# Deeper weight splitting in the up product of a hybrid encoder layer, and three reorderings around it

## The chip, the cores and the metric

The kernel runs on one core of a Trainium2 chip. The metric is the device time of one launch in microseconds (us), lower is better. A core has five engines that work side by side, each through its own queue in program order: TensorE (PE; its weight loads are shown as PEld), VectorE (DVE, `V` in the code), ScalarE (ACT, `A`), GpSimd (POOL, `G`) and SyncE (SP), which here issues nearly all DMAs. An engine that waits for something holds up all that stands behind it in its queue.

## The reference

One layer of an encoder trunk is applied to two batches (prompt and sample) of 512 tokens of width 1024, with shared weights, all in float32:

```python
xn = _rmsnorm(x, norm1_g); proj = xn @ w_in
a_out = (gelu(lru_gate) * (h_fwd + h_bwd)) @ w_lru_out      # RG-LRU in both directions
b_out = o.reshape(B, S, ATT_OUT) @ w_att_out                # dilated window attention, three groups
x = x + (sigmoid(g_a) * a_out + sigmoid(g_b) * b_out) @ w_o
xn2 = _rmsnorm(x, norm2_g)
gate, val = jnp.split(xn2 @ w_up, 2, axis=-1)
x = x + (gelu(_dwconv(gate, ffn_conv_w, ffn_conv_b)) * val) @ w_down
```

w_up is 1024 x 6144, w_down 3072 x 1024, w_o 1024 x 1024.

## The kernel before

**Split weights.** A product of float32 matrices is made of three matmuls of a faster type: every operand is split into a high part (hi, a cast) and a low part (lo, the difference), and hi*hi, hi*lo and lo*hi are added up in a PSUM bank. A weight slab (128 x 512, 256 KB) is loaded into a raw buffer (four of them) by SP, its hi is cast by ACT (L227) and its lo subtracted by an engine from the list `lo_eng` (L230), which is rotated at each split. hi and lo have eight buffers each.

**The stream.** All slabs stand in one list, in the order of their use, and the class `Stream` (L64) hands them out. `adv(n)` splits up to n more slabs, as long as fewer than eight are live; `take(n)` gives n to the caller and splits them first if it must; `done` says that n are used up. Loads are issued three places ahead of the splits. Since every engine works in program order, the place at which `adv` stands in the code fixes where the cast, the subtraction and the load stand in the queues of ACT, DVE or POOL, and SP. `hold` stops the splits at a given slab until it is raised.

**The stages around the change.** After the input projections and attention come, for batch 0 and then batch 1:

- mix (`mix_tile`, L985): eight tiles; each takes three slabs of w_lru_out and one of w_att_out, multiplies 30 + 12 matmuls into a double bank (two such banks), and DVE multiplies the gates on (L1000 to L1004). Gates come by `th_load` one tile ahead. The rows of x, onto which the output is added, come by `load_acc` (four DMAs of 512 KB): for batch 0 ahead of the mix, for batch 1 after its tile 3.
- output (`o_phase`, L1056, `o_group`, L1041): 16 groups of 12 matmuls, each added to the rows by DVE (L1054, called the residual's addition here). In batch 0 a hook after each group also splits batch 1's y (L846, L847), transposes its o (L886 to L889) and, in the last four groups, makes the second norm: `norm2_tile` (ACT squares, POOL takes the root, DVE scales by L1020 into an `x2s` buffer) and two groups later `norm2_T`, whose transposes give the operands B11 and B21 (L1037 to L1039).
- the last eight groups of batch 1 (L1173) have their own norm steps between them, in the table `after` (L1162): `own_sums` (store the rows, ACT squares them into a PSUM bank called junk), `own_scale`, and `sums`, whose transposes (L1122) and additions give the operands T1 to T4 and B22. In the last two of these groups each slab is given back as soon as it is used, and the first eight slabs of w_up are split there.

**The up product.** w_up's columns go in 24 steps f of 128 gate and 128 value columns, and seven products (Strassen's scheme in Winograd's form) do the work of eight: B11 and B21 (`batch0`, L1205), then T2, T1, T3, B22 and T4 (`rest`, L1218), 12 matmuls each (`prod`, L1188; matmuls L1195 to L1197). Their slabs are A11, A12, S2, S1, S3, S4, A22, of which four come from additions on DVE in `up_split` (L257): S1 = A21 + A22, S2 = S1 - A11 when A12 is split (for f < 4 when S2 is), S3 = A11 - A21 and S4 = A12 - S2, written over A21 and A12, when S2 is split. A21 has one buffer, A22 two, S1 and S2 one each. T2, T3 and T4 are added up in one bank (pfA), T1 and B22 in another (pfC); between T2 and T3 the bank is copied (u2, by ACT at L1229, for f = 2 and 3 by DVE), between T1 and B22 likewise (p5), and after T3 DVE adds it to p5 (L1236). After B22 come the gate (g1), a convolution over the tokens on DVE (L1243, L1245), gelu on ACT (L1247), two multiplications on DVE and the store f_d. For f < 4 B11 and B21 run ahead, while `sums` of the last rows is still under way; these are the `batch0(0)` to `batch0(3)` in front of the loop. After `batch0(2)` `hold` is raised and lo goes to POOL alone.

**The down product** follows (L1314 to L1316); at its start the first two f rows are fetched and split (`h_pair`, L1265), and rows of x come back from DRAM (accd).

Of the kernel before, what the change touches and what calls it, by code (L numbers as in the profile page):

```python
# [11 lines left out]
F32 = mybir.dt.float32  # L12
# [7 lines left out]
D = 1024  # L20
T = 1024
S = 512
# [91 lines left out]
def layer_kernel(ctx: ExitStack, tc: tile.TileContext, xs_in, norm1_g, w_in, conv_w, conv_b, lru_wa, lru_ba,  # L114
# [3 lines left out]
    V, A, G, PE, SP = nc.vector, nc.scalar, nc.gpsimd, nc.tensor, nc.sync  # L118
# [3 lines left out]
    def open_pool(name, side="left", **kw):  # L122
        cm = tc.tile_pool(name=name, bufs=1, side=side, reuse_waits="tile", **kw)
        return cm, cm.__enter__()
# [83 lines left out]
    hi_eng, lo_eng = ["dve"], [G]  # L208
# [69 lines left out]
    ws = Stream(specs, wload, wsplit, 3, {"a": 8, "b": 8})  # L278
# [3 lines left out]
    def wcol(slabs, j):  # L282
        return lambda k: slabs[k // 4][j][:, 128 * (k % 4):128 * (k % 4) + 128]
# [17 lines left out]
    for t in range(8):  # L301
        x_t = xi.tile([128, D], F32, name=f"xt{t}")
# [653 lines left out]
    cm_ps, ps3 = open_pool("ps3", space=PSUM)  # L956
# [3 lines left out]
    cm_m, mp = open_pool("mix")  # L960
# [3 lines left out]
    def load_acc(b):  # L964
        for i in range(4):
            acc[4 * b + i] = acp.tile([128, D], F32, tag=f"acc{i}", bufs=1, name="acc")
            SP.dma_start(out=acc[4 * b + i], in_=xs_in[b][0, 128 * i:128 * i + 128, :])
# [4 lines left out]
    def half_pair(pool, nm, **kw):  # L972
        return tuple(pool.tile([128, 4, S], F32R, name=nm, tag=nm + hl, bufs=1) for hl in "hl")
# [11 lines left out]
    def mix_tile(b, c):  # L985
        wa = ws.take(3)
        ps = ps3.tile([128, 2, 512], F32, tag="m", bufs=2, name="ps")
        mm3(ps[:, 0], wcol(wa, 0), wcol(wa, 1), lambda k: yh[k], lambda k: yl[k], KR)
        ws.done("a", 3)
        ws.adv(2)  # L990
        wb = ws.take(1)
        mm3(ps[:, 1], wcol(wb, 0), wcol(wb, 1), lambda k: oT["h"][:, k], lambda k: oT["l"][:, k], 4)
        ws.done("a", 1)
        ws.adv(2)
        if c + 1 < KD:
            th_load(b, c + 1)
        ta, tb = ths.pop((b, c, 0)), ths.pop((b, c, 1))
        mh = mbp.tile([128, S], F32R, tag=f"mh{c}", bufs=1, name="mh")
        ml = mbp.tile([128, S], F32R, tag=f"ml{c}", bufs=1, name="ml")
        V.scalar_tensor_tensor(out=ta, in0=ta, scalar=1.0, in1=ps[:, 0], op0=ALU.add, op1=ALU.mult)  # L1000
        V.scalar_tensor_tensor(out=tb, in0=tb, scalar=1.0, in1=ps[:, 1], op0=ALU.add, op1=ALU.mult)
        V.tensor_tensor(out=ta, in0=ta, in1=tb, op=ALU.add)
        act(out=mh, in_=ta, func=AF.Copy, scale=0.5)
        V.scalar_tensor_tensor(out=ml, in0=ta, scalar=0.5, in1=mh, op0=ALU.mult, op1=ALU.subtract)  # L1004
        mix[c] = (mh, ml)
# [17 lines left out]
    SP.dma_start(out=gain2, in_=norm2_g[0].partition_broadcast(128))  # L1023

    def norm2_tile(t):
        x_t = mp.tile([128, D], F32, tag="x2s", bufs=2, name="x2s")
        norm2_scale(t, x_t, norm2_sums(t, x_t), gain2)
        xst[t] = x_t

    def norm2_T(t):  # L1030
        x_t = xst.pop(t)
        tl = slice(128 * (t % 4), 128 * (t % 4) + 128)
        for kk in range(0, KD, 4):
            h, l = x2["B11" if kk == 0 else "B21"]
            pst = ps3.tile([128, 4, 128], F32, tag="t", bufs=4, name="pst")
            for j in range(4):
                PE.transpose(out=pst[:, j], in_=x_t[:, 128 * (kk + j):128 * (kk + j) + 128], identity=ident)  # L1037
            A.copy(out=h[:, :, tl], in_=pst)
            V.tensor_tensor(out=l[:, :, tl], in0=pst, in1=h[:, :, tl], op=ALU.subtract)  # L1039

    def o_group(t, kq, hlf, w4, free=False):  # L1041

        tl = slice(128 * (t % 4), 128 * (t % 4) + 128)
        cl = slice(512 * hlf, 512 * hlf + 512)
        ps = ps3.tile([128, 512], F32, tag="t", bufs=4, name="pso")
        for k in range(4):
            mh, ml = mix[4 * kq + k]
            PE.matmul(out=ps, lhsT=mh[:, tl], rhs=w4[k][0], start=(k == 0), stop=False)
            PE.matmul(out=ps, lhsT=mh[:, tl], rhs=w4[k][1], start=False, stop=False)
            PE.matmul(out=ps, lhsT=ml[:, tl], rhs=w4[k][0], start=False, stop=(k == 3))  # L1050
            if free:
                ws.done("a", 1)
                ws.adv(1)
        V.tensor_tensor(out=acc[t][:, cl], in0=acc[t][:, cl], in1=ps, op=ALU.add)  # L1054

    def o_phase(b, hook, orders):  # L1056
# [6 lines left out]
            ws.done("a", 4)  # L1063

    th_load(0, 0)
    load_acc(0)
    ws.adv(8)
    for c in range(KD):
        mix_tile(0, c)
    x2["B11"], x2["B21"] = half_pair(x20p, "B11"), half_pair(x20p, "B21")  # L1070
    ystage, ostage = {}, {}
    new_oT()

    def hook0(n, i):
        if 1 <= n <= KR:
            y_split(n - 1, ystage.pop(n - 1))
        if n < KR:
            ystage[n] = mp.tile([128, S], F32, tag="yst", bufs=2, name="yst")
            SP.dma_start(out=ystage[n], in_=y_d[128 * n:128 * n + 128, :])
        if n < 4:  # L1080
            ostage[n] = mp.tile([128, S], F32, tag="ost", bufs=2, name="ost")
            SP.dma_start(out=ostage[n], in_=o_d[128 * n:128 * n + 128, :])
        if 1 <= n <= 4:
            o_transpose(n - 1, ostage.pop(n - 1), ps3, "t")
        if i is not None:
            norm2_tile(i)
            store_acc(i)
            if i >= 2:
                norm2_T(i - 2)

    o_phase(0, hook0, O_ORDER)
    th_load(1, 0)
# [16 lines left out]
    def own_sums(i):  # L1109

        store_acc(4 + i)
        rs_own[i] = norm2_sums(4 + i, ps3.tile([128, D], F32, tag="m", bufs=2, name="junk"))

    def own_scale(i):
        norm2_scale(4 + i, acc[4 + i], rs_own.pop(i), gain2)
# [37 lines left out]
    def sums(i, pool=None, tag=None):  # L1153

        if i not in pieces:
            pieces[i] = sums_T(i, pool.tile([128, 2, 512], F32, tag=tag, bufs=2 if tag == "m" else 1, name="pst"))
        next(pieces[i])
# [6 lines left out]
        3: lambda: (own_sums(1), own_scale(0)),  # L1164
        4: lambda: (own_scale(1), sums(0, ps3, "m")),
        5: lambda: (own_sums(2), sums(0)),
        6: lambda: (own_scale(2), sums(1, ps3, "m"), sums(0)),
        7: lambda: (own_sums(3), sums(1), own_scale(3)),
    }
    for n, (i, hlf) in enumerate(((0, 0), (1, 0), (0, 1), (1, 1), (2, 0), (2, 1), (3, 0), (3, 1))):  # L1170
        if n == 2:
# [16 lines left out]
    def prod(ps, slab, op, start, free=True):  # L1188

        wh, wl = slab  # L1190
        bh, bl = x2[op]
        for k in range(4):
            a = wh[:, 128 * k:128 * k + 128]
            kw = dict(skip_group_check=True)
            PE.matmul(out=ps, lhsT=a, rhs=bh[:, k], start=(start and k == 0), stop=False, **kw)  # L1195
            PE.matmul(out=ps, lhsT=a, rhs=bl[:, k], start=False, stop=False, **kw)
            PE.matmul(out=ps, lhsT=wl[:, 128 * k:128 * k + 128], rhs=bh[:, k], start=False, stop=(k == 3), **kw)  # L1197
        if free:
            ws.done("a", 1)
            ws.adv(1)  # L1200

    bank = lambda nm: (ps4 if nm == "C" else ps4ab).tile([128, 512], F32, tag=nm, bufs=2, name="pf" + nm)
    row = lambda nm, bufs=1: fp.tile([128, S], F32, tag=nm, bufs=bufs, name=nm)
# [159 lines left out]
```

## Time and profile before

| | |
|---|---|
| median of three runs | 2146.39 us (2146.15 to 2147.89) |
| the profiled execution: its own time | 2148.48 us |
| the profiled execution: span of its instructions | 2146.70 us |
| mean granted TensorE clock | 0.984 of full speed |
| PE busy | 2043.2 us, 95% of the span |
| PEld busy | 1707.9 us, 80% |
| DVE busy | 1254.0 us, 58% |
| ACT busy | 872.0 us, 41% |
| POOL busy | 745.8 us, 35% |
| DMA engines | 31.8% by SP's queue, 102 GB/s in the mean |

The page gives busy time by engine, the span in 40 slices, the costliest groups of instructions by line with what ended the idle time before them, and the chain of work that ended last. Busy shares are means over stages with different limits; so the stages are read one by one, in the timeline, where each instruction has its start, its length and, in brackets, the time for which its engine stood idle before it and what ended that.

### The profile page before, as it was taken

How to read it: one execution, taken by the hardware profiler on the slowest of the kernel's cores; microseconds unless marked ns; L12 is line 12 of the kernel's file. 1: busy time of each engine (PE TensorE's matmuls, PEld its weight loads, DVE VectorE, ACT ScalarE, POOL GpSimd, SP SyncE). 2: the span in 40 equal slices, each digit the busy share in tenths (PEclk: the TensorE clock that was granted, in tenths of full speed). 3: DMA queues.
4: the chain of work that ended last, by engine and by line, in shares of the span. 5: the costliest groups of instructions: out<-in, count | busy, mean ns of one | idle time of the engine just before them, and what ended most of it. 6: DMA issues, size and time to landing. Idle time of an engine off the chain costs nothing.

```text
span 2146.7 us, 26423 instructions
## 1 busy us (share of the span) xinstructions
PE 2043.2 (95%) x9571; PEld 1707.9 (80%) x9571; DVE 1254.0 (58%) x1833; ACT 872.0 (41%) x1501; POOL 745.8 (35%) x624
## 2 busy tenths in 40 slices
PE   8989889999999999999999999889999999899999
PEld 6867667787899999998778778667777777688887
DVE  5599998527862671674563532655544545555555
ACT  4488888522431242145433332433334334421210
POOL 3111111034213422423346344554445445442331
PEclk9999999999999999999999999999999999999999
DMA  4535444511111111104447455322222222252322
GB/s 145 154 98 141 126 121 122 161 45 40 39 43 43 41 52 50 30 26 147 158 163 223 156 178 157 108 69 89 79 69 89 76 72 89 103 212 88 107 90 79
DMA packets 204032, 218.71 MB, mean 102 GB/s; under 512 B 28892, under 2 KB 148222, under 8 KB 203902
## 3 DMA queue, kind: packets, MB, share of 16 engines
q1 hardware_dynamic: 201854, 211.78, 31.8%
q0 software_dynamic: 2048, 5.25, 1.0%
q8 instruction: 75, 1.23, 0.2%
q14 instruction: 55, 0.45, 0.1%
HBM read 161.73 MB, written 50.00 MB: 99 GB/s over the span
## 4 chain that ended last, share of the span: by engine, by line
PE 54%; issue 19%; DVE 10%; POOL 10%; ACT 4%; DMA 2%; SPq 0%; POOLq 0%; DVEq 0%; ACTq 0%
POOL lo L230 8%; PE ps L807 7%; PE ps L808 6%; PE ps L809 6%; PE psd L1315 4%; PE psd L1316 4%; PE psd L1314 4%; PE ps L151 4%; PE ps L152 4%; PE ps L153 4%; DVE u L486 3%; PE o L728 3%; PE sp L691 2%; DVE u L478 1%; PE pt L715 1%
## 5 line engine op out<-in xcount | busy, mean ns | idle before, releaser
L230 POOL TENSOR_TENSOR lo<-raw,hi 128x512 fp32r<-128x512 f32 (+1 forms) x302 | 386.0, 1289 | 672.0 <-ACT hi L227 637.0
L227 ACT CAST hi<-raw 128x512 fp32r<-128x512 f32 (+1 forms) x352 | 206.7, 606 | 275.4 <-PE psd L1316 155.7
L807 PE MATMUL ps<-hi,xh 128*128 128x512 f32 x576 | 251.4, 437 | 0.0
L808 PE MATMUL ps<-lo,xh 128*128 128x512 f32 x576 | 228.5, 397 | 0.0
L809 PE MATMUL ps<-hi,xl 128*128 128x512 f32 x576 | 228.3, 396 | 0.0
L151 PE MATMUL ps<-xh,hi 128*128 128x512 f32 x544 | 217.7, 400 | 0.3 <-DVE xc L403 0.3
L152 PE MATMUL ps<-xl,hi 128*128 128x512 f32 x544 | 216.3, 398 | 0.0
L153 PE MATMUL ps<-xh,lo 128*128 128x512 f32 x544 | 215.5, 396 | 0.0
L1317 DVE TENSOR_TENSOR accd<-accd,psd 128x512 f32<-128x512 f32 x192 | 130.8, 686 | 117.7 <-PE psd L1316 111.7
L807 PEld LDWEIGHTS ps<-hi,xh 128*128 128x128 f32 x576 | 156.1, 271 | 9.6
L808 PEld LDWEIGHTS ps<-lo,xh 128*128 128x128 f32 x576 | 158.3, 275 | 6.0
L809 PEld LDWEIGHTS ps<-hi,xl 128*128 128x128 f32 x576 | 156.4, 272 | 7.9
L1314 PE MATMUL psd<-hi,hp 128*128 128x512 f32 x384 | 150.5, 392 | 2.5 <-ACT hi L227 2.5
L1315 PE MATMUL psd<-lo,hp 128*128 128x512 f32 x384 | 150.7, 393 | 1.6 <-POOL lo L230 1.6
L1316 PE MATMUL psd<-hi,hp 128*128 128x512 f32 x384 | 150.5, 392 | 0.0
L707 ACT ACTIVATE p<-p,nm 128x128 f32<-128x128 f32 (+1 forms) x192 | 81.7, 427 | 146.3 <-DVE nm L705 146.3
L629 DVE TENSOR_REDUCE ss<-sq 128x8 f32<-128x512 f32 x48 | 32.9, 685 | 163.7 <-ACT sq L626 163.7
L151 PEld LDWEIGHTS ps<-xh,hi 128*128 128x128 f32 x544 | 105.0, 193 | 24.7 <-issue 1.4
L153 PEld LDWEIGHTS ps<-xh,lo 128*128 128x128 f32 x544 | 104.7, 192 | 22.7
L152 PEld LDWEIGHTS ps<-xl,hi 128*128 128x128 f32 x544 | 104.9, 193 | 22.0
L1197 PE MATMUL pfA<-T,lo 128*128 128x512 f32 x288 | 112.3, 390 | 3.4 <-POOL lo L230 3.4
L1195 PE MATMUL pfA<-T,hi 128*128 128x512 f32 x288 | 112.3, 390 | 1.3 <-ACT hi L227 1.3
(255 smaller groups left out, 4518.0 us busy)
## 6 DMA issues: line engine op xcount, KB each, us to landing
raw<-in_w_in_dram SPq DMA_DIRECT2D x144, 256.0 KB
raw<-in_w_up_dram SPq DMA_DIRECT2D x56, 256.0 KB
r<-in_w_up_dram SPq DMA_DIRECT2D x48, 256.0 KB
f_d<-gc SPq DMA_DIRECT2D x24, 512.0 KB
hraw<-f_d SPq DMA_DIRECT2D x24, 512.0 KB
raw<-in_w_down_dram SPq DMA_DIRECT2D x48, 256.0 KB
sg_d<-sgt SPq DMA_DIRECT2D x16, 512.0 KB
raw<-in_w_lru_out_dram SPq DMA_DIRECT2D x32, 256.0 KB
```

What stands on the lines that cost most here:

```text
L151: PE.matmul(out=ps, lhsT=a, rhs=b, start=(k == 0), stop=False)
L152: PE.matmul(out=ps, lhsT=a, rhs=rl(k), start=False, stop=False)
L153: PE.matmul(out=ps, lhsT=wl(k), rhs=b, start=False, stop=(k == n - 1))
L227: A.copy(out=hi[:, 0:n], in_=r[:, 0:n])
L230: e.tensor_tensor(out=lo[:, 0:n], in0=r[:, 0:n], in1=hi[:, 0:n], op=ALU.subtract)
L807: PE.matmul(out=ps, lhsT=a, rhs=hi, start=(k == 0), stop=False)
L808: PE.matmul(out=ps, lhsT=a, rhs=lo, start=False, stop=False)
L809: PE.matmul(out=ps, lhsT=b, rhs=hi, start=False, stop=(k == KD - 1))
L1314: PE.matmul(out=ps, lhsT=hh[:, i, tl], rhs=w[0], start=(i == 0), stop=False)
L1315: PE.matmul(out=ps, lhsT=hh[:, i, tl], rhs=w[1], start=False, stop=False)
L1316: PE.matmul(out=ps, lhsT=hl[:, i, tl], rhs=w[0], start=False, stop=(i == 1))
L1317: V.tensor_tensor(out=acc[t][:, cl], in0=acc[t][:, cl], in1=ps, op=ALU.add)
```

## The change

It has five parts.

- `prod`: after each product `adv(2)` in place of `adv(1)`.
- The last two groups of batch 1's output: the slabs are given back as before, but nothing is split inside the group; four splits stand behind the addition of the seventh group, and four behind the norm steps of the eighth, for which DVE is first taken off `lo_eng`.
- `lo_eng` is set to DVE and POOL in turn ahead of batch 0's mix, and no longer POOL alone up to the last groups.
- `load_acc(0)` moves from before the mix to behind its tile 3.
- In batch 0's hook the y and o loads share one ring of three buffers (two rings of two before), `norm2_T(i - 2)` stands ahead of `norm2_tile(i)`, and `x2s` has three buffers for two.

```diff
     def norm2_tile(t):
-        x_t = mp.tile([128, D], F32, tag="x2s", bufs=2, name="x2s")
+        x_t = mp.tile([128, D], F32, tag="x2s", bufs=3, name="x2s")
...
             if free:
                 ws.done("a", 1)
-                ws.adv(1)
         V.tensor_tensor(out=acc[t][:, cl], in0=acc[t][:, cl], in1=ps, op=ALU.add)
...
     th_load(0, 0)
-    load_acc(0)
+    lo_eng[:] = [V, G]
     ws.adv(8)
     for c in range(KD):
         mix_tile(0, c)
+        if c == 3:
+            load_acc(0)
...
         if n < KR:
-            ystage[n] = mp.tile([128, S], F32, tag="yst", bufs=2, name="yst")
+            ystage[n] = mp.tile([128, S], F32, tag="yst", bufs=3, name="yst")
             SP.dma_start(out=ystage[n], in_=y_d[128 * n:128 * n + 128, :])
         if n < 4:
-            ostage[n] = mp.tile([128, S], F32, tag="ost", bufs=2, name="ost")
+            ostage[n] = mp.tile([128, S], F32, tag="yst", bufs=3, name="ost")
             SP.dma_start(out=ostage[n], in_=o_d[128 * n:128 * n + 128, :])
         if 1 <= n <= 4:
             o_transpose(n - 1, ostage.pop(n - 1), ps3, "t")
         if i is not None:
+            if i >= 2:
+                norm2_T(i - 2)
             norm2_tile(i)
             store_acc(i)
-            if i >= 2:
-                norm2_T(i - 2)
...
-        6: lambda: (own_scale(2), sums(1, ps3, "m"), sums(0)),
-        7: lambda: (own_sums(3), sums(1), own_scale(3)),
+        6: lambda: (ws.adv(4), own_scale(2), sums(1, ps3, "m"), sums(0)),
+        7: lambda: (own_sums(3), sums(1), own_scale(3), lo_eng.remove(V), ws.adv(4)),
     }
...
         if free:
             ws.done("a", 1)
-            ws.adv(1)
+            ws.adv(2)
```

## Rows read from the trace of the kernel before

**Rows 1.** List of PE's waits, whole span: us in total, times, longest us.
```profile
PE pfB L1197 <- POOL lo L230: 13.5, 20, 0.7
```

**Rows 2.** Timeline, up product: start us, us, engine, line, operation [idle before].
```profile
1487.87 0.39 PE L1195 MATMUL pfA<-B,hi 128*128 128x512 f32 x1
...
1489.99 0.60 ACT L227 CAST hi<-raw 128x512 fp32r<-128x512 f32 x1
...
1492.06 0.50 PE L1197 MATMUL pfB<-B,lo 128*128 128x512 f32 x1 [0.69 <-POOL lo L230]
...
1494.46 0.39 PE L1195 MATMUL pfA<-T,hi 128*128 128x512 f32 x1
...
1497.18 0.39 PE L1195 MATMUL pfC<-T,hi 128*128 128x512 f32 x1
...
1851.34 0.39 PE L1195 MATMUL pfA<-B,hi 128*128 128x512 f32 x1
```

**Rows 3.** Timeline, start of batch 0's mix, 1120 to 1133.
```profile
1120.68 1.90 SPq L967 DMA_DIRECT2D acc<-in_x_prompt_dram  x4
...
1125.08 0.69 DVE L1000 SCALAR_TENSOR_TENSOR tha<-tha,ps 128x512 f32<-128x512 f32 x1 [7.72 <-DMA tha<-sg_d]
...
1126.73 0.47 PE L151 MATMUL ps<-yh,hi 128*128 128x512 f32 x1 [4.10 <-DVE thb L1001]
...
1132.08 0.62 ACT L227 CAST hi<-raw 128x512 fp32r<-128x512 f32 x1 [0.36 <-DMA raw<-in_w_att_out_dram]
```

**Rows 4.** Timeline, batch 0's output, the first pass.
```profile
1191.93 0.68 DVE L847 TENSOR_TENSOR yl<-yst,yh 128x512 fp32r<-128x512 f32 x1
...
1194.34 0.60 PE L886 MATMUL pt<-ident,ost 128*128 128x128 f32 x4
```

**Rows 5.** Timeline, end of batch 0's output, 1236 to 1244.
```profile
1236.86 1.28 DVE L1039 TENSOR_TENSOR B<-pst,B 128x512 fp32r<-128x512 f32 x2
...
1237.69 1.09 PE L1037 MATMUL pst<-ident,x2s 128*128 128x128 f32 x4 [3.54 <-DVE B L1039]
...
1243.27 0.63 PE L153 MATMUL ps<-yh,lo 128*128 128x512 f32 x1
```

**Rows 6.** Timeline, border of output and up product, 1369 to 1378.
```profile
1369.35 0.61 ACT L1147 CAST T<-acc 128x512 fp32r<-128x512 f32 x1
...
1370.52 1.60 DVE L230 TENSOR_TENSOR lo<-raw,hi 128x512 fp32r<-128x512 f32 x1 [1.72 <-ACT hi L227]
...
1374.36 0.67 DVE L1054 TENSOR_TENSOR acc<-acc,pso 128x512 f32<-128x512 f32 x1
...
1376.27 1.97 PE L1122 MATMUL pst<-ident,acc 128*128 128x128 f32 x8 [9.01 <-ACT junk L1014]
```

**Rows 7.** Timeline, up product, f = 0 to 3.
```profile
1405.53 1.28 POOL L230 TENSOR_TENSOR lo<-r,hi 128x512 fp32r<-128x512 f32 x1
...
1408.05 0.39 PE L1195 MATMUL pfA<-T,hi 128*128 128x512 f32 x1
...
1421.19 0.75 PE L1195 MATMUL pfC<-T,hi 128*128 128x512 f32 x1 [2.09 <-ACT hi L227]
...
1440.44 1.15 SPq L245 DMA_DIRECT2D r<-in_w_up_dram  x2
...
1445.64 0.69 DVE L259 TENSOR_TENSOR s<-r,r 128x512 f32<-128x512 f32 x1 [0.46 <-DMA r<-in_w_up_dram]
```

**Rows 8.** Timeline, f = 23 and the start of the down product.
```profile
1866.12 0.50 PE L1197 MATMUL pfA<-T,lo 128*128 128x512 f32 x1 [1.95 <-POOL lo L230]
...
1877.25 0.50 PE L1314 MATMUL psd<-hi,hp 128*128 128x512 f32 x1 [2.45 <-ACT hi L227]
...
1879.32 0.79 PE L1315 MATMUL psd<-lo,hp 128*128 128x512 f32 x1 [1.56 <-POOL lo L230]
...
1885.03 0.60 PE L1316 MATMUL psd<-hi,hp 128*128 128x512 f32 x1
```

**Rows 9.** Groups of instructions by line: busy us, mean ns, idle before.
```profile
L259 DVE TENSOR_TENSOR raw<-raw,s 128x512 f32<-128x512 f32 x24 | 39.4, 1640 | 0.0
```

## The prediction

> **What bounds the kernel now.** TensorE is busy 95% of the span, so a change can only win where it stands still, and I read the list of its waits first. The most frequent is the up product waiting for POOL's lo half: 20 waits of 0.7 us [rows 1], once per round of the f loop. The timeline of one round shows how [rows 2]: B11 starts at 1487.87, and T2, two products later, at 1494.46, 6.59 us for two products, where one product takes 2.72 (1494.46 to 1497.18). So B21 loses 1.15 us. Why: its slab A12 is split only two products ahead, and its cast stands in ACT's queue behind the gelu, running at 1489.99; the lo follows on POOL, and B21's third matmul waits for it until 1492.06. From 1487.87 (f = 5) to 1851.34 (f = 23) are 18 rounds, 20.19 us each; seven products of 2.72 are 19.04. The difference is again 1.15. The other stops are single ones at stage borders, and I look at each below in the timelines of all engines.
>
> All times are of the profiled execution, 2148.48 us with a span of 2146.70; the median of the runs is 2146.39, 2.09 lower, and a difference from the one is carried to the other. A change of 0.2% (4.3 us) is about what a measurement can tell.
>
> **The f loop, rounds 4 to 22.** A product frees one slab and may now split two. From two slabs the lead grows by one per product until all eight buffers are full; then each product splits the slab eight places on. A12's cast is then issued in the round before, no longer behind the gelu that precedes its use. What it costs: a cast now reuses the slab just freed, so it waits for TensorE's end of that product and the eviction copy behind it on ACT comes 0.6 us later [rows 2]; that copy has one product, 2.72, of slack. On DVE the adds S1, S2 move behind the gate's multiplications, and g0 behind S3, S4; g0 is read only after B22, 10 us on. The load of A21 has a single buffer and waits for the lo of S3 before it; S3's cast now follows the fourth product of the round before (10.9 us in), so the lo ends near 12.8. The adds come 23 us after that round's start, behind its gate multiplications, and a load takes 5.2 [rows 7], so 5 us are left over. DMA and POOL do the same work as before. Gain 19 x 1.15 = 21.9 (15 to 23).
>
> **Its beginning, f = 0 to 3.** Here running ahead costs. In T2 of f = 0 the second split is already S2 of f = 1. It needs A21 of f = 1, whose load waits for the lo of S3 of f = 0, ending near 1406.8 [rows 7]. Two such loads, issued at 1440.44, let the adder go at 1445.64: 5.2 us. So 1412.0 for the data, two adds of 0.7, the cast 0.6: 1414.0. The copy u2 of f = 0 stands behind that cast on ACT, done at 1414.6, and T3 may not write over the bank before it: 1414.6 in place of 1408.05, 6.6 us. After a stop of that length TensorE runs at its lower clock for a while [rows 5], 2 us more; and POOL now does S1's lo and two lo halves that DVE did before, 1.6 us more in front. That is 10.2. In return the casts behind the gelu, which make T1 of the next f wait (2.09 at 1421.19), come earlier, and lead to waits at T3 and T4 in their place that I put at about 3.6 less over f = 1 to 3. Loss 6.6 net (0, if the load lands sooner than in that row, to 14, if the stop repeats at f = 1).
>
> By the Trainium skill, page SBUF — State Buffer, section Who interferes with whom, a DVE instruction with two inputs in SBUF and a GpSimd instruction that reads SBUF block each other for the whole instruction. This trace agrees in kind: the S4 add takes 1.64 us in the mean [rows 9] and 0.69 is what an add takes alone [rows 7]. It speaks against splitting two slabs per product while DVE adds; what it would do is the third rival.
>
> **Its end.** In f = 23 the cast of S3 and its lo stand behind the first pair's preparation: T3 waits 1.95. The down product then waits 2.45 and 1.56 for slabs that nobody had split, and after that its matmuls come 0.43 apart instead of 0.23, some 14 of them, 2.8 us, the last at 1885.03 [rows 8]. With eight slabs ahead these are split before T4. New there: u2 of f = 23 waits behind casts that wait for the fetched f rows, about 1. With B21 of f = 23 (1.15) that makes 9 (4 to 10.5); next late are the residual rows, which land when the eighth bank is wanted.
>
> **Splits after the residual.** Now the last two groups of the output product issue four splits before their addition. DVE stands at 1370.52 and again before 1374.36 for casts whose loads are late, the addition runs at 1374.36, the norm's square behind it, and the transposes of the next stage, which take its bank, start at 1376.27 after 9.01 us [rows 6]. With the addition ahead, DVE does it when its earlier work ends, at 1368.8 (1370.52 less the 1.72 that it then waits), and ACT the square after the cast at 1369.35, which ends at 1369.96. From the addition's end, 1375.03, to the transposes are 1.2 us now; so they start at 1371.2. Gain 5.1; the lower clock after the stop stays, since 3.9 us of it do. Eight casts and eight lo move behind an addition of 0.7. Of the last four, two lo go from DVE to POOL, 2.6 us there, covered until T2 of f = 0, where I counted them. I take 5 (3 to 8).
>
> **lo on two engines, rows of x later.** From the mix on, some 40 lo move from POOL (1.3 us) to DVE (0.7), beside matmuls that wait for none of them. One place is not covered: the first mix tiles. DVE's addition for tile 0 waits for the gates until 1125.08, and TensorE for its bank until 1126.73. In the new order the lo of slab att02 stands ahead of that addition on DVE, and its cast ran at 1132.08, because four 512 KB loads of x sat in the queue at 1120.68 [rows 3]. These four move on SP's queue behind tile 3, past sixteen slab loads and eight gate loads. Between the first gate's landing and the slab's, some 7.0 us, lie 2.69 MB with these four, 384 KB per us; without them 0.64 MB, 1.7 us. That puts the slab at 1126.8; with the cast 0.6, the lo 0.7 and two gate steps of 0.7 the bank is free at 1129.5, 2.8 later than now. The ends are +8, if the slab comes as late as now, and -1, if the gates land sooner; nearest to the row's own rate, and with the end's wait for POOL gone, I take +2, and -1 to 5 for the range. The moved loads come where batch 1 has its own, and no wait of TensorE stands there.
>
> **One ring for y and o.** Three buffers in place of two pairs: o's second load must now wait for the first y's subtraction, which ends at 1192.6, and its transposes are wanted at 1194.34 [rows 4]. Between nothing and 3.5 us (5.2 less 1.7) for each of two such loads; I take 1.5 in all (0 to 3), since these loads are half as large.
>
> **Transposes before the norm.** At the end of batch 0, DVE's subtractions at 1236.86 stand behind the scale of a later row, and transposes wait 3.54 us for their bank; a dozen matmuls up to 1243.27 then come 0.43 apart [rows 5], 2.6 us. In the new order eight transposes, two casts and two subtractions pass the square, POOL's root and the scale of the later row; the square waits for the two casts, at most 1.1, and the scale with it, which nothing wants before the next tile is through. SP's store stays behind. The third buffer lets the square write without waiting for those transposes. Gain 3.5 alone, 6.2 with the clock; I take 5.5.
>
> **Sum.** -21.9 + 6.6 - 9 - 5 + 2 + 1.5 - 5.5 = -31.3: 2148.5 becomes 2117.2, and against the median 2115.1, **2115 us**.
>
> **Rivals.** *The loop's wait comes back in another place* (u2 or the additions, since ACT and DVE serve casts first): for it, every cast now waits for its product; against it, 2 us of slack in my walk. Then the 21.9 are lost: 2137. *Loads that land later than they are used*, the slower end: in every round u2 stands behind the cast of S2, which hangs on one buffer for A21. The stop that I expect at f = 0 would then stay in all rounds. It decides from 10.5 us per load on, twice the 5.2 of [rows 7], and the kernel is slower if a round takes over 20.7 us; at one product lost per round it is 2115 + 20 x 2.72 = 2169. Against it: the f loop gives a load seven products' time, f = 0 only five, and traffic there is low. *Adds and lo block each other*: in the beginning each of two adds ahead of a cast takes 1.64 and the lo behind it wait too, some 2.5 us in each of f = 0 to 2: 2122. That is the result by the Trainium skill's page on SBUF — State Buffer, Who interferes with whom. *It doesn't run ahead*, because loads come only three specs early: then the f loop, its beginning and its end stay as they are and -5 + 2 + 1.5 - 5.5 = -7 is left: 2139, by their bounds 2131 to 2146, so that half of it is no change that can be told.
>
> **Chances.** Forecast 0.62; loop's wait elsewhere 0.12; blocking 0.12; late loads 0.08; not ahead 0.06. The forecast's own bounds, not all at one end, give 2104 to 2126; with 2122 and 2137 inside, 2104 to 2138 leaves out less than 2 in 10. Faster 0.62 + 0.12 + 0.12 + 0.03 = 0.89, slower 0.08, the same 0.03.
>
> **What would show it.** Rounds of 19.0 to 19.1 us with no wait of pfB for POOL; T3 of f = 0 waiting some 6 us for ACT; the down product starting without a wait; the transposes ahead of the up product at 5 us earlier after the residual; the pause of 3.54 at the norm gone; in the mix a pause of some 7 us, not shorter than now. I am wrong if rounds stay over 19.6, if every T3 waits for ACT, or if the stop at f = 0 passes 12 us.

## The result and the profile after

The changed kernel takes 2123.65 us in the median, against 2146.27 for the kernel before in the same series of runs: ratio 0.9887 (95% interval 0.9868 to 0.9907), 1.1% faster. One of the four runs, which took 2852.98 us at a granted clock of 0.655, is counted in the median and left out of the ratio; the other three took 2120.09 to 2123.89. 2115 was forecast, and the range was 2104 to 2138. The profiled execution takes 2123.89 us (span 2122.1), 24.6 less than the profiled one of before; 31.3 were forecast.

The line numbers of the changed kernel are one lower or higher than before: L1196 to L1198 are the matmuls of `prod`, L1230 copies u2, L1123 transposes the last rows, L1315 to L1317 are the down product. First its page, the engines' busy time:

```profile
PE 2032.0 (96%) x9571; PEld 1710.5 (81%) x9571; DVE 1296.6 (61%) x1874; ACT 873.1 (41%) x1501; POOL 691.7 (33%) x583
```

41 lo halves have moved from POOL to DVE. The list of PE's waits over the whole span (us in total, times, longest us) shows where TensorE stands now:

```profile
PE ps L151 <- DVE thb L1001: 9.0, 1, 9.0
PE pfA L1196 <- ACT u L1230: 9.0, 3, 3.6
...
PE pst L1123 <- ACT junk L1014: 5.0, 1, 5.0
...
PE pfA L1196 <- ACT hi L227: 3.8, 1, 3.8
...
PE pfA L1196 <- DVE u L1228: 2.0, 1, 2.0
...
PE pst L1123 <- DVE B L1128: 1.8, 1, 1.8
```

The 20 waits of pfB for POOL [rows 1] are gone, as are the stop at the norm [rows 5] and those at the start of the down product [rows 8]. New are the waits for u. The one of T2 of f = 0 for a hi half has grown from 1.3 to 3.8; in the list of before it is this line:

```profile
PE pfA L1195 <- ACT hi L227: 1.3, 1, 1.3
```

The one ahead of the mix has doubled, from 4.1 to 9.0 [rows 3]. The timeline of all engines (start, length, engine, line, operation, in brackets the idle time before and what ended it) shows each place:

```profile
1126.86 0.62 ACT L227 CAST hi<-raw 128x512 fp32r<-128x512 f32 x1 [0.35 <-DMA raw<-in_w_att_out_dram]
1127.51 0.69 DVE L230 TENSOR_TENSOR lo<-raw,hi 128x512 fp32r<-128x512 f32 x1 [8.28 <-ACT hi L227]
1128.12 0.68 DVE L1000 SCALAR_TENSOR_TENSOR tha<-tha,ps 128x512 f32<-128x512 f32 x1
...
1129.54 0.77 PE L151 MATMUL ps<-yh,hi 128*128 128x512 f32 x1 [8.97 <-DVE thb L1001]
...
1366.97 0.68 DVE L1053 TENSOR_TENSOR acc<-acc,pso 128x512 f32<-128x512 f32 x1
...
1369.33 1.91 PE L1123 MATMUL pst<-ident,acc 128*128 128x128 f32 x8 [5.05 <-ACT junk L1014]
...
1397.24 1.14 ACT L227 CAST hi<-s 128x512 fp32r<-128x512 f32 x2 [3.93 <-DVE s L259]
...
1397.91 0.79 PE L1196 MATMUL pfA<-T,hi 128*128 128x512 f32 x1 [3.83 <-ACT hi L227]
...
1402.90 1.28 POOL L230 TENSOR_TENSOR lo<-r,hi 128x512 fp32r<-128x512 f32 x1
...
1404.21 0.92 SPq L245 DMA_DIRECT2D r<-in_w_up_dram  x2
...
1407.92 0.69 DVE L259 TENSOR_TENSOR s<-r,r 128x512 f32<-128x512 f32 x1 [6.76 <-DMA r<-in_w_up_dram]
...
1409.37 0.62 ACT L227 CAST hi<-s 128x512 fp32r<-128x512 f32 x1 [7.63 <-DVE s L259]
...
1409.89 0.58 ACT L1230 COPY u<-pfA 128x512 f32<-128x512 f32 x1
...
1410.53 0.80 PE L1196 MATMUL pfA<-T,hi 128*128 128x512 f32 x1 [3.56 <-ACT u L1230]
...
1417.94 0.69 DVE L259 TENSOR_TENSOR s<-r,r 128x512 f32<-128x512 f32 x1 [2.08 <-DMA r<-in_w_up_dram]
...
1420.48 0.68 DVE L1239 TENSOR_TENSOR g<-u,pfC 128x512 f32<-128x512 f32 x1
...
1426.78 1.06 ACT L1248 ACTIVATE gc<-gc 128x1024 f32<-128x1024 f32 x1
...
1428.77 0.57 ACT L1230 COPY u<-pfA 128x512 f32<-128x512 f32 x1
...
1429.40 0.50 PE L1196 MATMUL pfA<-T,hi 128*128 128x512 f32 x1 [3.46 <-ACT u L1230]
...
1842.63 1.05 ACT L1272 CAST hp<-hraw 128x1024 fp32r<-128x1024 f32 x1 [3.53 <-DMA hraw<-f_d]
...
1845.39 0.58 ACT L1230 COPY u<-pfA 128x512 f32<-128x512 f32 x1
...
1846.02 0.50 PE L1196 MATMUL pfA<-T,hi 128*128 128x512 f32 x1 [1.96 <-ACT u L1230]
```

The reader sees five things. In the mix the lo half ends at 1128.2 and the addition for tile 0 stands behind it on DVE. The residual's addition is done early, at 1367.65. T2 of f = 0 then waits for the cast of S2. T3 of f = 0 waits for u2, and u2 stands behind a cast whose sums wait for a load that was issued at 1404.21, just after the lo of S3. In f = 1 the same wait comes by a detour: the sums of f = 2 wait for their load in front of the gate of f = 0, so the gelu of f = 0 ends at 1427.84, and u2 of f = 1 stands behind it.

For a ledger the span is cut at eight instructions that every kernel has: **G**, the transposes of o that end TensorE's stop of 2.1 us for POOL's cg (1044.99 before); **M**, the matmul that ends the stop ahead of the mix (1126.73); **O**, the last matmul ahead of the residual's stop (1366.88); **R**, the transposes that end it (1376.27); **T2** of f = 0 (1400.51); **B4** and **B23**, the first matmul of B21 in f = 4 and f = 23 (1470.51 and 1854.12); **D**, the first matmul of the down product (1873.96); **L**, the last matmul (2142.31). Differences of their starts, in us:

| kernel | G | G-M | M-O | O-R | R-T2 | T2-B4 | B4-B23 | B23-D | D-L |
|---|---|---|---|---|---|---|---|---|---|
| before | 1044.99 | 81.74 | 240.15 | 9.39 | 24.24 | 70.00 | 383.61 | 19.84 | 268.35 |
| after | 1044.42 | 85.12 | 234.35 | 5.44 | 28.58 | 76.07 | 361.76 | 20.20 | 261.80 |
| quiet | 1045.47 | 85.56 | 234.40 | 5.46 | 28.41 | 72.77 | 365.35 | 18.66 | 261.56 |
| u2first | 1043.98 | 85.09 | 234.06 | 5.46 | 28.55 | 76.48 | 361.76 | 18.41 | 261.55 |
| only2 | 1046.98 | 81.68 | 238.81 | 9.58 | 24.91 | 74.29 | 361.76 | 18.90 | 261.56 |
| nores | 1044.68 | 84.96 | 235.14 | 9.60 | 23.73 | 77.06 | 361.76 | 20.66 | 261.56 |
| slow | 1044.41 | 85.25 | 233.68 | 5.45 | 28.37 | 67.95 | 361.76 | 19.00 | 261.57 |
| mixlo | 1044.68 | 82.07 | 234.65 | 5.42 | 28.53 | 74.46 | 361.76 | 18.64 | 261.80 |
| lastlo | 1045.27 | 85.79 | 234.10 | 5.46 | 30.58 | 77.07 | 361.76 | 20.44 | 261.56 |
| hpair | 1047.74 | 85.43 | 233.97 | 5.46 | 28.40 | 75.83 | 361.76 | 18.11 | 264.58 |
| lead3 | 1042.60 | 85.51 | 234.56 | 5.45 | 28.39 | 67.76 | 361.76 | 18.01 | 265.84 |
| normfirst | 1045.01 | 85.21 | 240.58 | 5.44 | 28.40 | 76.73 | 361.76 | 20.32 | 261.75 |
| best | 1044.99 | 81.66 | 234.68 | 5.45 | 28.40 | 67.20 | 361.76 | 18.79 | 261.78 |
| best2 | 1042.82 | 81.94 | 234.15 | 5.45 | 28.46 | 68.26 | 361.76 | 18.89 | 261.56 |

No kernel changes anything ahead of G, and yet it moves between 1042.60 and 1047.74; so the ledger carries the argument, and single times of a kernel differ by up to 6 us (nores: 2120.86 to 2126.81). In the loop (B4-B23) nothing moves: 19 rounds of 19.04 in every run with the change but quiet.

The ledger has a chance of its own wherever TensorE stops for some 2 us. In eleven of the profiled executions T3 of f = 23 waits 1.71 to 2.44 us for u2. In four of them (after, nores, lastlo, normfirst) some eight matmuls at the lower level of TensorE's clock follow, 1.6 us in all; in the other seven none does, after waits as long. Two of them in the view of windows, over the 4.6 us from the start of T3 (us, busy time and count by engine, granted clock, DMA share, GB/s), the changed kernel and slow:

```profile
1846.00:1850.60 4.60, 4.58 (x13) 3.67 (x14) 0.04 (x1) 1.60 (x3) 3.89 (x3) 0.64 0.50 183
1837.60:1842.20 4.60, 4.60 (x20) 3.82 (x21) 0.69 (x1) 1.73 (x3) 4.60 (x4) 1.00 0.43 158
```

The wait is 1.96 in the first and 2.37 in the second. So a difference of 1.6 us in B23-D is no effect of an edit by itself.

### The profile page after: what moved, and what is told of

Same layout as the page of the kernel before. It is cut to its first block, busy times and chain, and to the rows that moved or that the text cites. A ratio compares the mean times of both kernels' runs of the same rounds, so it can differ in the third digit from the quotient of the medians.

```text
span 2122.1 us, 26424 instructions
## 1 busy us (share of the span) xinstructions
PE 2032.0 (96%) x9571; PEld 1710.5 (81%) x9571; DVE 1296.6 (61%) x1874; ACT 873.1 (41%) x1501; POOL 691.7 (33%) x583
## 4 chain that ended last, share of the span: by engine, by line
PE 75%; DVE 12%; issue 4%; ACT 4%; POOL 2%; DMA 2%; SPq 0%; DVEq 0%; POOLq 0%; ACTq 0%
PE ps L807 7%; PE ps L808 6%; PE ps L809 6%; PE ps L151 5%; PE ps L152 5%; PE ps L153 5%; PE psd L1315 4%; PE psd L1317 4%; PE psd L1316 4%; PE pfA L1196 4%; PE pfA L1197 3%; PE pfA L1198 3%; DVE u L486 3%; PE o L728 3%; PE pfC L1196 2%
## 5 line engine op out<-in xcount | busy, mean ns | idle before, releaser
L230 POOL TENSOR_TENSOR lo<-raw,hi 128x512 fp32r<-128x512 f32 (+1 forms) x261 | 344.6, 1331 | 668.1 <-ACT hi L227 635.4
L1315 PE MATMUL psd<-hi,hp 128*128 128x512 f32 x384 | 149.7, 390 | 0.4 <-DVE gc L1255 0.4
L1317 PE MATMUL psd<-hi,hp 128*128 128x512 f32 x384 | 149.4, 389 | 0.0
L1196 PE MATMUL pfA<-T,hi 128*128 128x512 f32 x288 | 116.0, 403 | 15.4 <-ACT u L1230 9.0
L1198 PE MATMUL pfA<-T,lo 128*128 128x512 f32 x288 | 115.3, 400 | 0.9 <-POOL lo L230 0.9
```

The costliest lines, as they stand in the source:

```text
L230: e.tensor_tensor(out=lo[:, 0:n], in0=r[:, 0:n], in1=hi[:, 0:n], op=ALU.subtract)
L1315: PE.matmul(out=ps, lhsT=hh[:, i, tl], rhs=w[0], start=(i == 0), stop=False)
L1317: PE.matmul(out=ps, lhsT=hl[:, i, tl], rhs=w[0], start=False, stop=(i == 1))
```

## The experiments

Each is the changed kernel with one edit, but for only2 (an edit of the kernel before), best and its variant. Ratios are to the kernel before in the same series of runs.

### Where the beginning of the f loop loses

**quiet** holds back the second split until f = 4.

```diff
-            ws.adv(2)
+            ws.adv(step[0])
...
+    step = [1]
...
     for f in range(NF):
...
+        if f == EARLY:
+            step[0] = 2
```

> The changed kernel, but a product of the up stage splits one slab until f = 4 begins, and two from then on. Theory (in f = 0 to 3 running ahead costs, because the copy of u2 stands behind the cast of the next f's S2, which waits for A21's load): the two stops of T3 for ACT (3.56 and 3.46 us in f = 0 and 1) and the one of 2.04 in f = 3 are gone, the waits of T1 that the kernel before has (2.09 and two of about 1.4) come back, rounds from f = 5 on stay at 19.04; about 2118 us. Rival (what is lost there is POOL's backlog from batch 0's preparation, with additions and lo halves that slow each other): T3 of f = 0 still waits over 2 us and the time stays at 2122 to 2124.

Measured: 2125.16 us (ratio 0.9894, 0.9879 to 0.9909): no gain. The stops of f = 0 to 3 are gone as expected (T2-B4 is 3.3 shorter), and they are paid again in f = 4: B4-B23 is 3.6 longer, all of it in its first two rounds (22.27 and 19.40). Both theories missed this. The timeline of quiet shows the new place:

```profile
1482.23 1.80 DVE L259 TENSOR_TENSOR s<-r,r 128x512 f32<-128x512 f32 x1 [4.30 <-POOL lo L230]
...
1486.00 0.50 PE L1197 MATMUL pfC<-B,hi 128*128 128x512 f32 x1 [1.85 <-ACT p L1236]
```

There the sums wait again, now in f = 4, and the p5 copy is late behind their cast. The profile puts the wait down to POOL, but the loads of A21 and A22 were issued at 1478.51, right behind the lo of S3 (ended 1478.48), and the sums start 3.72 us later, as long as such loads take in the changed kernel at f = 0 (1404.21 to 1407.92). So the loss goes with the rounds in which the lead grows, here as there.

**u2first** takes away what stands between T2 and its copy.

```diff
-        prod(pa, ws.take(1)[0], "T2", early)
+        prod(pa, ws.take(1)[0], "T2", early, free=False)
...
             A.copy(out=u2, in_=pa)
+        ws.done("a", 1)
+        ws.adv(2)
```

> The changed kernel, with the copy (or addition) that makes u2 issued ahead of the splits that T2 frees, and nothing else moved. Theory (only the order on ACT and DVE makes T3 wait; the data that the cast waits for are not wanted before the next f): the waits of T3 in f = 0, 1, 3 and 23 (3.56, 3.46, 2.04, 1.96 us) and the low clock behind them (1.6 to 2.3 us each) are gone, 2112 us, 2108 to 2117. Rival (loads of A21 land late, so the wait only moves to T1 or T2 of the next f, where a hi half is then missing): waits for the cast hi of over 5 us in all in f = 1 to 3, and 2120 or more.

Measured: 2120.37 us (0.9872, 0.9858 to 0.9887), but T2-B4 is 76.48, no shorter. The wait of f = 0 moves on to the p5 copy, and the one of f = 1 grows:

```profile
1410.95 0.50 PE L1196 MATMUL pfC<-B,hi 128*128 128x512 f32 x1 [1.70 <-ACT p L1237]
...
1427.70 0.58 ACT L1230 COPY u<-pfA 128x512 f32<-128x512 f32 x1
...
1428.34 0.80 PE L1196 MATMUL pfA<-T,hi 128*128 128x512 f32 x1 [6.21 <-ACT u L1230]
```

The rival was right that the wait only moves, though not as to where: no hi half is missing, u2 of f = 1 stands behind the late gelu of f = 0. B23-D is 1.8 shorter, but T3 of f = 23 still waits 1.71 (1.96 before the edit); the rest is that no slow matmuls follow this time, which is the chance described above. The time itself can't be told from the changed kernel's (0.9868 to 0.9907).

**slow** lets the lead grow by one slab per f.

```diff
-            ws.adv(2)
+            ws.adv(2 if op == "B22" else 1)
```

> The changed kernel, but only the product B22 splits two slabs, the others one: the lead grows by one slab per f instead of one per product. Theory (what costs is the speed at which the lead grows: six extra slabs within six products, while one buffer for A21 lets one f's sums be made per load; it moved to f = 4 where the growth was put there): no stop of T3 for ACT over 1 us in f = 0 to 3, the wait of T1 of f = 1 (2.09 in the kernel before) is gone since its cast is issued before the gelu, from T2 of f = 0 to B21 of f = 4 62 to 67 us (70.0 before, 76.07 in the changed kernel), rounds of 19.04 from f = 5 on, 2111 to 2116 us. Rival (a second split in any product that stands ahead of an eviction makes T3 wait): stops of some 3 us return in f = 0 to 3, 2120 to 2124.

Measured: 2114.80 us (0.9846, 0.9832 to 0.9861), inside the theory's range; T2-B4 takes 67.95, just over the 62 to 67 expected, 8.1 less than in the changed kernel (5.7 of it in waits, the rest in slow matmuls behind them) and 2 less than before. What is left, by the list of PE's waits:

```profile
PE pfA L1196 <- ACT u L1230: 3.7, 2, 2.4
PE pfA L1196 <- DVE p L1237: 2.1, 1, 2.1
```

2.37 of the first is the wait in f = 23; the other 1.30 is T3 of f = 1, which the theory had at under 1, and the second line is T4 of f = 1. So it isn't running ahead that costs. What limits it is in the trace of the changed kernel: the sums of each f need A21, which has one buffer, and each pair of its loads is issued right behind the lo of S3 (1404.21 behind 1404.18, 1414.18 behind 1414.15, 1429.72 behind 1429.69). That the rate of growth costs, and not its place, isn't shown apart: slow also puts every second split behind B22, away from the copies that ACT makes, and a growth of one slab per f placed behind T2 wasn't run. For the rate speaks u2first, where the splits that T2 frees stand behind u2 and the loss stays.

**lead3** gives the loop one slab more than before, and no more.

```diff
-            ws.adv(2)
+            ws.adv(extra.pop(op, 1))
...
+    extra = {"B22": 2}
```

> The changed kernel, but one slab is split per product except in the first B22, where it is two: the lead is three slabs from f = 0 on and never more. Theory (the f loop gains because one cast is issued ahead of the gelu instead of behind it, for which one slab more of lead is enough): rounds of 19.04 without a wait of pfB for POOL; the end, where the lead of eight covered the start of the down product, loses 2 to 6 us against the run that grows to eight: 2117 to 2121. Rival (the loop needs the eight buffers): rounds over 19.6 and 2127 or more.

Measured: 2116.57 us (0.9847, 0.9830 to 0.9863), a little faster than expected. The rounds are 19.04 from f = 4 on, so the whole gain of the loop hangs on one slab more, by which the cast of A12 stands ahead of the gelu on ACT (at 1511.7, the gelu at 1519.83; before, the gelu at 1509.22 and the cast at 1510.19). The end lacks the lead, by the list of PE's waits:

```profile
PE psd L1316 <- ACT hi L227: 1.9, 1, 1.9
...
PE psd L1317 <- POOL lo L230: 0.9, 1, 0.9
```

B23-L is 283.85 here and 280.57 in slow: the eight buffers are worth some 3 us, at the start of the down product alone.

### What the residual's part brings

**nores** splits in the last two groups as before.

```diff
             if free:
                 ws.done("a", 1)
+                ws.adv(1)
...
-        6: lambda: (ws.adv(4), own_scale(2), sums(1, ps3, "m"), sums(0)),
-        7: lambda: (own_sums(3), sums(1), own_scale(3), lo_eng.remove(V), ws.adv(4)),
+        6: lambda: (own_scale(2), sums(1, ps3, "m"), sums(0)),
+        7: lambda: (own_sums(3), sums(1), own_scale(3)),
```

> The changed kernel with the output product's last two groups as before: four splits each ahead of their addition, lo halves alternating. Theory (what the earlier addition won, 3.95 us at the transposes, is nearly all given back before T2 of f = 0, because POOL and DVE are behind there): same time within 2 us, 2123 to 2126, TensorE waits 9 us ahead of the transposes and about 1.3 ahead of T2 of f = 0. Rival (the gain stays to the end): 2127 to 2129.

Measured: 2125.22 us (0.9890, 0.9872 to 0.9908), the same as the changed kernel. O-R takes 9.60 in place of 5.44, but R-T2 23.73 in place of 28.58: from O to T2 of f = 0 33.33 against 34.02. The gain of 4 us at the transposes is all given back before T2. The timeline of the changed kernel shows where:

```profile
1376.09 6.37 POOL L230 TENSOR_TENSOR lo<-raw,hi 128x512 fp32r<-128x512 f32 x4
...
1386.36 0.62 ACT L1148 CAST T<-acc 128x512 fp32r<-128x512 f32 x1 [6.54 <-POOL acc L1128]
...
1387.98 0.69 DVE L1128 TENSOR_TENSOR acc<-pst,B 128x512 f32<-128x512 f32 x1 [5.45 <-ACT B L1132]
```

The four lo halves of the last splits, all on POOL now, stand ahead of its subtractions for T4 of the second last rows. ACT's cast of T4 waits for these, and behind that cast stand ACT's copies for the last rows, for which DVE waits; the sums of f = 0 come behind DVE's work on these rows. In nores POOL has no lo halves there, and the same cast runs at 1386.50, no later, although the transposes start 5.05 us later.

**lastlo** spares POOL two lo halves there.

```diff
-        7: lambda: (own_sums(3), sums(1), own_scale(3), lo_eng.remove(V), ws.adv(4)),
+        7: lambda: (own_sums(3), sums(1), own_scale(3), ws.adv(4), lo_eng.remove(V)),
```

> The changed kernel, but the last four splits of the output product still alternate their lo halves between DVE and POOL. Theory (POOL is behind in batch 0 of the up product, 2.6 us of it by these two lo halves): the waits of T2 of f = 0 (3.83 and 0.94) fall by 1.5 to 2.6 us; 2121 to 2122. Rival (DVE's own additions set that time): they stay at 4.5 to 5 us.

Measured: 2126.58 us (0.9899, 0.9882 to 0.9916). The waits at T2 fall from 4.8 to 2.7, as the theory has it, but a stop at the transposes of the last rows grows from 1.8 to 3.6, and O to T2 takes 36.04, 2.0 more. By the list of PE's waits and by the timeline of DVE:

```profile
PE pst L1123 <- DVE B L1128: 3.6, 1, 3.6
```

```profile
1374.90 3.48 DVE L230 TENSOR_TENSOR lo<-raw,hi 128x512 fp32r<-128x512 f32 x2
```

So moving those two lo halves wins nothing: on DVE they stand ahead of its work on the second last rows, for which the transposes of the last rows wait, as on POOL they stand ahead of POOL's. That the preparation of these rows' operands sets the time of T2 is what the two runs and their timelines point to. A kernel that holds the last splits back until it is done wasn't run.

### One part at a time

**only2** is the kernel before with `ws.adv(2)` in `prod` and nothing else.

> The kernel before with one edit: two splits per product of the up stage. Theory (the terms add up): loop -21.9, end -6.2, beginning about +5 to +6.5: 2123 to 2125 us, rounds of 19.04, T3 of f = 0 waits about 3.5 us. Rival (the loss in the beginning comes from the splits that now follow the residual's addition): the beginning costs 1 or less, 2118 to 2119.

Measured: 2125.06 us (0.9896, 0.9881 to 0.9911): the theory's 2123 to 2125, with two of its terms off. The loop gains 21.85 as expected; B23-L gains 7.73 for 6.2 (the wait in f = 23 has no slow matmuls behind it here), and T2-B4 loses 4.29, less than the 5 to 6.5, though T3 of f = 0 waits 5.37 and not 3.5. This one line has the whole gain of the change; the other four parts together can't be told from nothing in the time, since in the ledger they work against each other: against only2 the changed kernel has 3.4 more in G-M and 4.5 less in M-O.

**mixlo** sends lo halves to DVE only after the first mix tile.

```diff
     th_load(0, 0)
-    lo_eng[:] = [V, G]
...
         mix_tile(0, c)
+        if c == 0:
+            lo_eng[:] = [V, G]
```

> The changed kernel, with lo halves going to DVE only after the first mix tile. Theory (the lo of the fourth slab of the next tile stands ahead of the first tile's addition on DVE): TensorE's stop ahead of the mix falls from 9 to about 4.5 us, the restart comes 2.8 us earlier against the start of the gates' normalisation, some 2121 us. Rival (the addition waits for the gates, whose loads now share the queue with slabs): the stop begins later and ends at the same time, no gain.

Measured: 2120.57 us (0.9874, 0.9859 to 0.9889). G-M is 82.07 in place of 85.12, 3.05 less, as the theory has it. (T2-B4 and B23-D are 1.6 less each as well, in code that the edit doesn't touch.) The timeline:

```profile
1124.98 0.69 DVE L1000 SCALAR_TENSOR_TENSOR tha<-tha,ps 128x512 f32<-128x512 f32 x1 [7.39 <-DMA tha<-sg_d]
...
1126.75 0.49 PE L151 MATMUL ps<-yh,hi 128*128 128x512 f32 x1 [3.90 <-ACT hi L227]
```

The addition runs as soon as its gate lands. That is at 1124.98, as early as with the loads of x in the queue [rows 3], so moving these brings the addition no sooner.

**normfirst** puts norm, store and transposes of batch 0 back in their old order.

```diff
+            norm2_tile(i)
+            store_acc(i)
             if i >= 2:
                 norm2_T(i - 2)
-            norm2_tile(i)
-            store_acc(i)
```

> The changed kernel, with norm, store and transposes of batch 0 in the old order; the third buffer of the norm rows stays. Theory (the order makes the gain): a stop of over 3 us ahead of the transposes at the end of batch 0's output product returns, with matmuls some 0.2 us further apart behind it, 3.5 to 6.2 us more: 2127 to 2130. Rival (the third buffer makes it): no stop over 1 us there, 2123 to 2125.

Measured: 2129.03 us (0.9906, 0.9891 to 0.9920). M-O is 6.23 longer, with the old stop, by the list of PE's waits:

```profile
PE pst L1037 <- DVE B L1039: 3.4, 1, 3.4
```

So the order makes the gain, 6.2 here. What the ring and the third buffer cost between them can't be told from nothing: 234.35 + 6.23 is 0.4 more than before (240.15), 1.8 more than only2 (238.81), whose stop is as long (3.53) with fewer slow matmuls behind it, and M-O differs by 1.5 among the runs with the new order (233.68 to 235.14).

**hpair** prepares the first pair of the down product behind the p5 copy of f = 23.

```diff
-        if f == NF - 1:
-            h_pair(0, (V, G))
         rest(f, pa)
...
             A.copy(out=p5, in_=pc)
+        if f == NF - 1:
+            h_pair(0, (V, G))
```

> The changed kernel, with the first pair of the down product prepared after the copy of p5 in f = 23 instead of ahead of T2. Theory (u2 of f = 23 stands behind casts that wait for the fetched f rows): T3 of f = 23 doesn't wait (1.96 and some 1.6 of low clock gone), the down product starts 3 us earlier, 2120 to 2121. Rival (then the pair's halves or the residual rows are late at the down product): the same time within 1 us is lost there as a wait of psd.

Measured: 2125.70 us (0.9899, 0.9885 to 0.9914): the rival. T3 of f = 23 doesn't wait and B23-D is 2.1 shorter, of which up to 1.6 can be the chance of the clock; D-L is 2.8 longer. By the list of PE's waits from 1840 to 1870:

```profile
PE psd L1315 <- DVE gc L1257: 1.8, 1, 1.8
PE pfC L1196 <- ACT p L1235: 1.4, 1, 1.4
```

### Together

**best** is slow and mixlo in one.

> The changed kernel with two edits together: only B22 splits two slabs, and lo halves go to DVE after the first mix tile. If the terms add: 2114.8 less 3 = 2112, 2109 to 2114. If what the mix wins is lost in a later stop: 2114 to 2116.

Measured: 2111.55 us (ratio 0.9825, 0.9810 to 0.9840), with G-M 81.66 and T2-B4 67.20: the two terms add, and the version is faster than both kernels.

**best2** adds the early u2 of u2first.

> The two edits together, and u2 made ahead of the split that T2 frees. If the stops of T3 that are left (1.30 in f = 1, 2.37 in f = 23) hang on that split alone: 2108 to 2110. If they hang on casts issued earlier: the same as without it, 2112.

Measured: 2111.89 us (0.9824, 0.9809 to 0.9839): no difference. T3 still waits 1.64 in f = 1 and 2.18 in f = 23, so these don't hang on that split. The timeline has u2 of f = 1 (1416.51) behind the gelu of f = 0, which ends at 1416.10, and one cast; u2 of f = 23 (1832.71) stands behind the two casts of the fetched f rows.

A second buffer for A21, the direct test of its load, was not tried.

## Why the prediction was right or wrong

The terms of the sum against the ledger:

| term | taken | measured | from |
|---|---|---|---|
| ahead of G | 0 | -0.6 | G |
| mix start | +2 | +3.4 | G-M |
| norm order, ring | -5.5 + 1.5 | -5.8 | M-O |
| residual | -5 | +0.4 | O-R and R-T2 |
| beginning of the loop | +6.6 | +6.1 | T2-B4 |
| f = 4 to 22 | -21.9 | -21.85 | B4-B23 |
| f = 23, down start | -9 | -6.2 | B23-D and D-L |
| sum | -31.3 | -24.6 | |

**The loop** was right to a tenth, and so was its reason: the cast of A12 behind the gelu. lead3 shows that it needs one slab more; the eight that the text counted up to aren't what it lives on. "2 us of slack" for the evictions held: no wait stands in rounds 4 to 22 of after.

**Its beginning** was right in the mechanism at f = 0; that the sum came out (6.1 for 6.6) is luck. The load took 3.7 us (1404.21 to 1407.92), not 5.2 (in the row that the 5.2 was read from, two more loads had been issued just ahead, at 1439.02), and T3 waits 3.56. But the stop repeats at f = 1 (3.46) and, on DVE, at f = 3 (2.04). The bound of 14 had the repeat in it; the walk missed how it comes, by the gate of f = 0 standing behind sums that wait. The waits in f = 1 to 3 were to fall by 3.6; they were 5.7 before (2.09, 0.82 and 1.30 for hi halves, and 1.46 for lo halves behind them) and are 6.1 now. And POOL's 1.6 "in front" lies ahead of T2, outside this row. Behind the stops TensorE is at its lower level for a while, as this view of windows shows (us, busy time and count by engine, granted clock, DMA share, GB/s):

```profile
1393.00:1465.00 72.00, 57.62 (x218) 45.02 (x217) 41.21 (x53) 26.00 (x42) 40.18 (x29) 0.88 0.27 81
1410.60:1413.20 2.60, 2.60 (x6) 2.10 (x7) 0.00 (x0) 2.43 (x5) 2.60 (x3) 0.50 0.03 6
...
1475.00:1550.00 75.00, 75.00 (x333) 62.10 (x332) 42.40 (x53) 31.05 (x51) 38.58 (x28) 1.00 0.28 85
```

0.50 is 1.2 GHz; some 1.5 us were lost so behind T3 of f = 0, where the text had 2.

**The residual** is the step that failed. "Eight casts and eight lo move behind an addition of 0.7 ... covered until T2 of f = 0": the transposes do start earlier, by 3.95 (5.1 forecast), but T2 doesn't, and the gain is gone. They aren't covered: the last four lo halves hold POOL for 6.37 us ahead of its part in the last rows' operands, on which T2 hangs. nores shows it: with the old order O to T2 takes the same time. The text followed the gain to the next wait (the transposes) and not to the one after it.

**The end** was mis-sized. The stops of 2.45 and 1.56 and their low clock went, 6.55 in D-L. But u2 of f = 23, taken at "about 1", waits 1.96 behind casts that wait for the fetched rows, with 1.6 of lower clock behind it; that gives back what B21 and T3 of f = 23 gained, and B23-D is 0.36 longer. The 1.6 is chance, as the ledger's note has it: in only2, with a wait of 2.25 and no slow matmuls behind it, the two columns gain 7.7. In the one other place tried, hpair's, the wait comes at the down product.

**The mix** came as described and at the time given: the slab's cast at 1126.86 (1126.8 forecast), the bank 2.8 us later than before. What was taken off for POOL's wait ahead of it was no credit: DVE sets the end, whenever TensorE arrives. That the bank came at the forecast 1129.5 has some luck in it, since G was 0.6 earlier.

**The norm** came to the upper end, 6.2: the lower clock behind the stop (0.50 from 1237.60 to 1243.50 before) goes with the stop; the share of the clock varies, since only2 has 0.76 behind the same stop. **The ring** shows no cost that can be told, where the text had 1.5: TensorE waits 0.6 once for a load of o.

**The rivals.** *The loop's wait elsewhere*, *doesn't run ahead*: excluded by rounds of 19.04. *Late loads*: sums wait for a load four times in after, 15.6 us in all, and all four in f = 0 to 3; the mechanism was real for as long as the lead grows, but not in every round. *Adds and lo block each other*: the sums that lead to the stop at f = 0 take 0.69 each, alone, since POOL waits for the same data. By the Trainium skill, page SBUF — State Buffer, section Who interferes with whom, DVE's adds with two inputs in SBUF and POOL's instructions that read SBUF would block each other. This trace agrees in kind for the sums of f = 0 (the S1 add at 1394.37 takes 1.16 and the S2 add behind it 1.64, beside POOL's subtractions), but these were as slow before (1.18 and 1.67), and they are not what the beginning lost.

## What to carry to other kernels

Buy lead slowly: work that runs ahead faster than its slowest single buffer allows makes the engine that prepares it stand in front of the evictions that TensorE needs now. One more slab per pass, split behind B22, cost nothing here; one more per product, 8 us against that. And ask how much lead the wait needs: one slab was enough for 21.85 of the gain. A stop that gets shorter is worth only what reaches the end; follow it past the next wait, for here 4 us at one border were all gone 28 us later.

## What the runs showed that was not expected

- The way in which the lead grows decides, not the lead: T2-B4 plus the loop takes 437.8 us at two slabs per product, 438.1 when that starts at f = 4, and 429.7 at one extra slab per f, split behind B22.
- A stop of TensorE of about 2 us costs its own length or nearly double, by chance: behind the 1.96 in f = 23 and the 2.04 in f = 3 of the changed kernel come eight matmuls each some 0.43 apart in place of 0.23, 1.6 us more; behind 2.37 in f = 23 of slow and 2.25 of only2 there are none.
- Stages ahead of the first edit differ by 5 us between executions of kernels that are the same up to there (G), while 18 rounds of the f loop repeat to 0.01 us.
